# Two transformer-like blocks on one core: SSM products side by side, its input projection without the norm, rotation tables by state tile, and the SSM spread over more of block 1's projections

## The chip, the cores and the metric

The kernel runs on one core of a Trainium2 chip, as one program. TensorE does the matrix products, VectorE and ScalarE the elementwise work, SyncE (SP) issues the DMAs; each engine works through its own list of instructions in order. The metric is the device time of one execution in microseconds (us). Times of single instructions are from one execution that the hardware profiler recorded.

## The reference

Two blocks follow each other on 256 positions of width 1024, in float32. Block 1 is a hybrid layer:

```
n = rmsnorm(h, g_mix)                       # h * rsqrt(mean(h^2)) * g_mix
z = n @ w_in                                # q, k, v of 12 heads; u (512 wide); two gates (1024 each)
attn_d = dilated_attention(q, k, v) @ w_attn_proj
y = gelu(s5_ssm(u, ...))                    # 32 groups of 16 channels, 64 complex states each
ssm_d = (y @ w_glu_a) * sigmoid(y @ w_glu_b)
h = h + (gate_attn * attn_d + gate_ssm * ssm_d) @ w_out
h = h + (silu(n2 @ w_ffn_gate) * (n2 @ w_ffn_up)) @ w_ffn_down
h = h + sigmoid(h @ w_ple_gate) * (p @ w_ple_proj)
```

The SSM takes `u` through a matrix B per group into complex states, runs `h[t] = a * h[t-1] + (B u)[t]` over the 256 positions with a complex `a` per state, and reads `Re(C h) + D u`. Block 2 has two layers on the result and on a second sequence of 256 positions (a convolution module, then attention, each with an MLP), with gains and shifts from a conditioning vector.

## The kernel before

**Three products for one.** A float32 weight chunk of 128 x 1024 is loaded by DMA (tiles `r...`), ScalarE rounds it to a high part (`h...`), VectorE subtracts for the low part (`l...`), and TensorE makes three fast products with the high and low part of the other operand (`mm3`). `Stream.block` hands out 128 x 128 pieces and loads and splits the next chunk when one is used up. The streams are named after what they feed: `u`, `qkv` (with the products `pq` and `pv`), `gates` (`pgt`), `mix` (`m`), and so on.

**Block 1 up to the mix.** `Norm("n1")` sums squares of x (`ssn`), brings them into a column (`pcn`), takes the inverse root on VectorE and spreads it over all partitions (`bcn`). `gain_norm` makes `n_x`, the normed x in two parts (`nt`, `nh`, `nl`). From it come `u` (four products `pu`), then per head slot j the projections `slot_proj(j)` and the attention `slot_attn(j)`, and the gates. The stage `mix` needs the attention's result (`oh`, `ol`) and, in two of its three products, the SSM's result (`yh`, `yl`).

**The SSM.** `prelude` makes the step factors and rotation angles on VectorE. `ssm()` makes tables of rotations `tabs` by doubling (`cmul`, with `cm` as temporaries), and for each quarter q of the states combines two tables to the rotation of each position (`E`). For each of four state tiles of 128 states it multiplies `u` by B (`pb`, 32 rows of TensorE, real and imaginary part into one PSUM bank), rotates (`ab`, `gg`), runs the recurrence as VectorE scans, and rotates back (`DF`). Products with C (`py`, 32 columns of TensorE for each state tile) sum up the quarter, and a gelu gives `y`. Products in brackets of `together` are handed out as one piece, so that those in different rows or columns of TensorE can run beside each other.

**What sets the order.** Nothing runs as it is written down. Each call is recorded with a priority that counts up, and `Recorder.schedule` hands out the instructions for each engine from a cost table: the earliest priority whose operands and buffers are there, in the planner's own clock. The order that comes out is fixed when the program is built. Buffers are by tag: `S` and `Q` in SBUF, the PSUM banks `mm` (2), `at` (2), `ax`, `md`, `py` and `sb`. A section can be given priorities spread over a stretch: `ssm_part.spread(z0, z0 + (rec.prio - z0) * SSM_END)` lays the SSM over the first 0.8 of the priorities from the first projection to the last gate, so that its VectorE work stands between the projections' chunk splits.

Of the kernel before, what the change touches and what calls it, by code (L numbers as in the profile page):

```python
# [16 lines left out]
AF = mybir.ActivationFunctionType  # L17
# [76 lines left out]
GATES, SSM_END = (0, 0, 4, 12), 0.8  # L94
QA, QS = 3, 0.2
WO = ("mm", "at", "py", "sb")
# [386 lines left out]
def two_blocks(ctx: ExitStack, tc: tile.TileContext, I, out):  # L483
# [5 lines left out]
    def slot(name, shape, dt=FT, tag="S"):  # L489
        return rec.tile(tag, shape, dt, name)  # L490
# [54 lines left out]
    def load_feat(name, src, n=8):  # L545
        f = Feat(name, n)
        for i, t in enumerate(f.t):
            SP.dma_start(out=t, in_=src[:, 4 * i:4 * i + t.shape[1]])
        return f

    x0 = load_feat("x0", I["x"])
    SP.dma_start(out=cst, in_=I["cst"])
    SP.dma_start(out=prm, in_=I["prm"])
    pos = const("pos", [128, 2], I32)
    SP.dma_start(out=pos, in_=I["pos"])
# [207 lines left out]
    start = rec.prio  # L763
    nm = Norm("n1")
    for k in range(8):
        nm.add(x0[k])

# [92 lines left out]
    prelude()  # L860
    V.tensor_copy(identb, ident)
    for g in range(3):
        mf = tmp("mf", (128, 384))
        SP.dma_start(out=mf, in_=I["mask"][:, g])
        V.tensor_copy(mskb[:, g], mf)
# [14 lines left out]
    def ssm():  # L880
# [4 lines left out]
        V.memset(tabs[:, 0, :, 0, :], 1.0)  # L885
        V.memset(tabs[:, 1, :, 0, :], 0.0)
        for k in range(4):
            n = 1 << k
            for ab in range(2 if k < 3 else 1):
                o = 16 * (4 * ab + k)  # L890
                pc_ = cs[:, None, o:o + 16].to_broadcast([128, n, 16])
                ps_ = sn[:, None, o:o + 16].to_broadcast([128, n, 16])
                cmul(tabs[:, 0, ab, n:2 * n], tabs[:, 1, ab, n:2 * n], tabs[:, 0, ab, 0:n], tabs[:, 1, ab, 0:n],
                     pc_, ps_, (128, n, 16), "w")
        for q in range(4):
# [4 lines left out]
            ta = [tabs[:, i, 0, :, sq].rearrange("p b s -> p s b")[:, :, None, :].to_broadcast(full) for i in range(2)]  # L900
            tb = [tabs[:, i, 1, 0:8, sq].rearrange("p a s -> p s a")[:, :, :, None].to_broadcast(full) for i in range(2)]
            cmul(E[0], E[1], tb[0], tb[1], ta[0], ta[1], full, "w")
            for s2 in range(2):
                DF = []
                for s in (2 * s2, 2 * s2 + 1):
                    st = 4 * q + s
                    r = 32 * s
                    pb = bank("pb", (128, 2, T), "sb")
                    for ri in range(2):
                        PE.matmul(pb[:, ri], Bm[r:r + 32, q, ri, :], u[r:r + 32, q], start=True, stop=True,  # L910
                                  tile_position=(r, 0))
# [49 lines left out]
    z0 = rec.prio  # L961
# [870 lines left out]
```

## Time and profile before

| what | value |
|---|---|
| three runs, median (lowest to highest) | 1453.74 us (1450.98 to 1456.24) |
| the profiled execution, its own time | 1453.37 us |
| its span in the trace | 1451.6 us |
| TensorE (PE) busy, share of the span | 97% |
| VectorE (DVE) busy | 76% |
| ScalarE (ACT) busy | 48% |
| mean granted TensorE clock | 0.996 |

The span is the time from the first to the last instruction of the trace; the run's time has 1.8 us more around it. PE's busy share counts a matmul from its start to its modelled end, so matmuls that wait in the pipe count as well; how many start in a stretch says more. Line numbers of the trace are all L479, the line of the helper that hands out the instructions, so the rows are told apart by tile names. In a name, what stands before the arrow is written and what stands behind it is read.

### The profile page before, as it was taken

What the parts mean: (1) busy time and instruction counts of PE and PEld (TensorE: products, weight loads), DVE (VectorE), ACT (ScalarE), POOL (GpSimd) and SP (SyncE); (2) the same over time, 40 slices, a digit from 0 to 9 for tenths busy, and PEclk for the clock granted to TensorE, in tenths of its full rate; (3) what the DMA queues carried; (4) which work ended last, traced back from release to release, by engine and by line L of the source; (5) the groups of instructions that cost most, each with busy time, mean ns of one, the idle gap of its engine ahead of it and who ended that gap; (6) DMA issues with size and microseconds to landing.
All of it is one profiled execution on the core that took longest, in us unless ns stands there. A gap on an engine that the chain in (4) does not pass through costs nothing.

```text
span 1451.6 us, 26536 instructions
## 1 busy us (share of the span) xinstructions
PE 1414.4 (97%) x10436; PEld 1252.8 (86%) x10436; DVE 1101.1 (76%) x2244; ACT 703.7 (48%) x1233; POOL 1.9 (0%) x20
## 2 busy tenths in 40 slices
PE   6999999999999998999899999999999999999999
PEld 5888789998999998786699777778788987999998
DVE  7999995779999998585587986655444799777543
ACT  4544555554544445542265333333432569587532
POOL 0000000000000000000000000000000000000000
PEclk9999999999999999999999999999999999999999
DMA  8744455655565664679545776644232330366663
GB/s 329 262 160 130 161 157 158 188 174 177 187 189 180 188 197 148 218 244 308 183 139 171 228 243 220 217 145 132 87 91 70 91 114 31 117 178 186 188 194 98
DMA packets 78508, 249.58 MB, mean 172 GB/s; under 512 B 8496, under 2 KB 19248, under 8 KB 78384
## 3 DMA queue, kind: packets, MB, share of 16 engines
q1 hardware_dynamic: 78384, 247.89, 54.3%
q8 instruction: 82, 1.34, 0.4%
q14 instruction: 42, 0.34, 0.1%
HBM read 245.76 MB, written 2.10 MB: 171 GB/s over the span
## 4 chain that ended last, share of the span: by engine, by line
PE 82%; DVE 8%; DMA 6%; ACT 2%; issue 1%; SPq 0%; DVEq 0%; ACTq 0%
PE pf L479 33%; PE pq L479 5%; PE pd L479 4%; PE fu L479 4%; PE fg L479 4%; DMA rmod<-in_w_mod_dram 3%; PE p L479 3%; PE pgt L479 3%; PE pv L479 2%; PE m L479 2%; PE pg L479 2%; PE pa L479 2%; PE pw L479 2%; PE pe L479 1%; DVE ma L479 1%
## 5 line engine op out<-in xcount | busy, mean ns | idle before, releaser
L479 DVE TENSOR_TENSOR lffb<-rffb,hffb 128x1024 fp32r<-128x1024 f32 x64 | 78.4, 1225 | 87.9 <-ACT hffb L479 87.1
L479 ACT ACTIVATE hffb<-rffb 128x1024 fp32r<-128x1024 f32 x64 | 67.9, 1062 | 148.2 <-PE pf L479 145.5
L479 ACT ACTIVATE hffa<-rffa 128x1024 fp32r<-128x1024 f32 x64 | 68.0, 1062 | 122.4 <-PE pf L479 113.9
L479 DVE SCALAR_TENSOR_TENSOR ccv<-ucc,prm,ccv 128x241 f32<-128x241 f32 (+14 forms) x240 | 114.0, 475 | 4.0
L479 PE MATMUL pf<-eul,hffb 128*128 128x512 f32 (+1 forms) x288 | 107.4, 373 | 1.2 <-DVE xc L479 0.9
L479 PE MATMUL pf<-el,hffa 128*128 128x512 f32 (+1 forms) x288 | 106.9, 371 | 1.1 <-ACT hffa L479 1.1
L479 PE MATMUL pf<-euh,lffb 128*128 128x512 f32 (+1 forms) x288 | 106.9, 371 | 0.0
L479 PE MATMUL pf<-eh,hffa 128*128 128x512 f32 (+1 forms) x288 | 106.5, 370 | 0.0
L479 PE MATMUL pf<-eh,lffa 128*128 128x512 f32 (+1 forms) x288 | 106.5, 370 | 0.0
L479 PE MATMUL pf<-euh,hffb 128*128 128x512 f32 (+1 forms) x288 | 106.2, 369 | 0.0
L479 DVE TENSOR_TENSOR lffa<-rffa,hffa 128x1024 fp32r<-128x1024 f32 x64 | 78.2, 1224 | 19.9 <-ACT hffa L479 19.5
L479 ACT ACTIVATE hpw<-rpw 128x1024 fp32r<-128x1024 f32 x48 | 50.8, 1059 | 85.7 <-PE pg L479 24.4
L479 ACT ACTIVATE hqkv<-rqkv 128x1024 fp32r<-128x1024 f32 (+1 forms) x52 | 51.6, 993 | 57.7 <-PE pq L479 27.6
L479 ACT ACTIVATE hgu<-rgu 128x1024 fp32r<-128x1024 f32 x44 | 46.7, 1060 | 65.1 <-PE fu L479 29.2
L479 DVE SCALAR_TENSOR_TENSOR ma<-rmod,cvec,ma 128x1024 f32<-128x1024 f32 x56 | 71.0, 1282 | 8.5 <-DMA rmod<-in_w_mod_dram 8.3
L479 DVE SCALAR_TENSOR_TENSOR xT<-pf,mods,xT 128x256 f32<-128x256 f32 x72 | 34.6, 482 | 56.0 <-PE pf L479 56.0
L479 DVE TENSOR_TENSOR lpw<-rpw,hpw 128x1024 fp32r<-128x1024 f32 x48 | 58.5, 1221 | 21.5 <-ACT hpw L479 21.2
L479 PE MATMUL pf<-zh,hffa 128*128 128x258 f32 x256 | 72.4, 283 | 0.0
L479 PE MATMUL pf<-zl,hffa 128*128 128x258 f32 x256 | 72.4, 283 | 0.0
L479 PE MATMUL pf<-zh,lffa 128*128 128x258 f32 x256 | 72.3, 282 | 0.0
L479 PE MATMUL pf<-zuh,hffb 128*128 128x256 f32 x256 | 72.0, 281 | 0.0
L479 PE MATMUL pf<-zul,hffb 128*128 128x256 f32 x256 | 71.8, 281 | 0.0
(568 smaller groups left out, 4827.8 us busy)
## 6 DMA issues: line engine op xcount, KB each, us to landing
rmod<-in_w_mod_dram SPq DMA_DIRECT2D x96, 512.0 KB, 4.6
rffa<-in_w_ffa_dram SPq DMA_DIRECT2D x64, 512.0 KB, 3.6
rffb<-in_w_ffb_dram SPq DMA_DIRECT2D x64, 512.0 KB, 3.6
rpw<-in_w_pw_dram SPq DMA_DIRECT2D x48, 512.0 KB, 4.5
rgu<-in_w_gu_dram SPq DMA_DIRECT2D x44, 512.0 KB, 4.1
rqkv<-in_w_qkv_dram SPq DMA_DIRECT2D x36, 512.0 KB, 4.3
rdown<-in_w_down_dram SPq DMA_DIRECT2D x22, 512.0 KB, 3.9
rgates<-in_w_gates_dram SPq DMA_DIRECT2D x16, 512.0 KB, 3.6
```

The lines of the kernel that those rows point to most:

```text
L479: getattr(getattr(self.nc, op.eng), fn)(*map(real, args), **{k: real(v) for k, v in kw.items()})
```

## The change

1. x is loaded in halves behind the parameters, the first `u` chunk between them. The gain alone (`xgt`) is applied to x, split in two (`xgh`, `xgl`), and the four `pu` products use that; each sum stays in its own bank (`mm` and `at`) until the norm's factor is there, copied to SBUF (`bcs`), and VectorE multiplies by it into `u`. `n_x` is still made for the other projections.
2. `prelude` and the masks get priorities spread over `PRE` = 110, and the SSM starts its spread `PRE` later and ends at 0.9 instead of 0.8.
3. `tabs` has the state tile as the outer and the position as the inner index.
4. The B products of two state tiles are handed out together, on two banks (`sb` and `py`) and two row groups; the C products of all four state tiles of a quarter are handed out together, on four column groups, once instead of twice.

```diff
-GATES, SSM_END = (0, 0, 4, 12), 0.8
+GATES, SSM_END = (0, 0, 4, 12), 0.9
+PRE = 110
+SSM_PB = ('sb', 'py')
...
-    x0 = load_feat("x0", I["x"])
-    SP.dma_start(out=cst, in_=I["cst"])
     SP.dma_start(out=prm, in_=I["prm"])
+    x0 = Feat("x0")
...
+    xg = Pair("xg")
+    st_u = Stream("u")
+    for i, t in enumerate(x0.t):
+        SP.dma_start(out=t, in_=I["x"][:, 4 * i:4 * i + 4])
+        first = st_u.block() if not i else first
+        if not i:
+            SP.dma_start(out=cst, in_=I["cst"])
+    SP.dma_start(out=pos, in_=I["pos"])
     nm = Norm("n1")
     for k in range(8):
+        t = tmp("xgt", (128, T))
         nm.add(x0[k])
+        ts(t, x0[k], pp("g_mix", k), None, OP.mult)
+        split(t, *xg[k])
+    bc = nm.rstd()
+    pus = []
+    for m in range(4):
+        p = bank("pu", (128, T), ("mm", "at")[m % 2])
+        pus.append(p)
+        for k, x in enumerate(xg.all()):
+            mm3(p, st_u.block() if m or k else first, x, k == 0, k == 7)
...
-    bc = nm.rstd()
     n_x = gain_norm(x0, lambda k: pp("g_mix", k), bc, "n")
-    st_u = Stream("u")
     u = slot("u", [128, 4, T])
+    bcs = tmp("bcs", (128, T))
+    A.activation(bcs, bc, AF.Copy)
     for m in range(4):
-        p = bank("pu", (128, T))
-        lin(p, st_u, n_x)
-        A.activation(u[:, m], p, AF.Copy)
+        tt(u[:, m], pus[m], bcs, OP.mult)
...
+    pre_part.spread(rec.prio, rec.prio + PRE)
...
-                cmul(tabs[:, 0, ab, n:2 * n], tabs[:, 1, ab, n:2 * n], tabs[:, 0, ab, 0:n], tabs[:, 1, ab, 0:n],
-                     pc_, ps_, (128, n, 16), "w")
+                cmul(tabs[:, 0, ab, :, n:2 * n], tabs[:, 1, ab, :, n:2 * n], tabs[:, 0, ab, :, 0:n],
+                     tabs[:, 1, ab, :, 0:n], pc_, ps_, (128, 16, n), "w")
...
-            ta = [tabs[:, i, 0, :, sq].rearrange("p b s -> p s b")[:, :, None, :].to_broadcast(full) for i in range(2)]
-            tb = [tabs[:, i, 1, 0:8, sq].rearrange("p a s -> p s a")[:, :, :, None].to_broadcast(full) for i in range(2)]
+            ta = [tabs[:, i, 0, sq, :][:, :, None, :].to_broadcast(full) for i in range(2)]
+            tb = [tabs[:, i, 1, sq, 0:8][:, :, :, None].to_broadcast(full) for i in range(2)]
...
+                pbs = [bank("pb", (128, 2, T), tg) for tg in SSM_PB]
+                with rec.together(2):
+                    for ri in range(2):
+                        for s in range(2):
+                            r = 32 * (2 * s2 + s)
+                            PE.matmul(pbs[s][:, ri], Bm[r:r + 32, q, ri, :], u[r:r + 32, q], start=True, stop=True,
+                                      tile_position=(r, 0))
...
-                with rec.together(4):
-                    for i, (ci, d, ri) in enumerate(((0, 0, 0), (1, 1, 1), (2, 1, 0), (2, 0, 1))):
-                        for s in range(2):
-                            o = 2 * s2 + s
-                            PE.matmul(py[32 * o:32 * o + 32], Cp[ci][:, 4 * q + o, :], DF[s][:, d, ri],
-                                      start=i == 0, stop=i == 3, tile_position=(0, 32 * o))
+            with rec.together(4):
+                for i, (ci, d, ri) in enumerate(((0, 0, 0), (1, 1, 1), (2, 1, 0), (2, 0, 1))):
+                    for o in range(4):
+                        PE.matmul(py[32 * o:32 * o + 32], Cp[ci][:, 4 * q + o, :], DF[o][:, d, ri],
+                                  start=i == 0, stop=i == 3, tile_position=(0, 32 * o))
...
-    z0 = rec.prio
+    z0 = rec.prio + PRE
```

Since the planner sets the order, the lists of instructions show where things went. On VectorE at the end of the SSM (`lgates` and `lmix` are low parts of gate and mix chunks, `yl` the low part of the SSM's last quarter), before:

```order
L479 TENSOR_TENSOR lgates_507_2803<-rgates_505_2616,hgates_506_2787 128x1024
L479 TENSOR_TENSOR yl_92_2817<-ya_2741,yh_90_2798 128x256
L479 TENSOR_TENSOR lgates_511_2844<-rgates_509_2666,hgates_510_2833 128x1024
L479 TENSOR_TENSOR ol_223_2872<-sp_2622,oh_221_2863 128x256
L479 TENSOR_TENSOR lgates_515_2884<-rgates_513_2699,hgates_514_2869 128x1024
L479 TENSOR_TENSOR lgates_519_2917<-rgates_517_2727,hgates_518_2903 128x1024
L479 TENSOR_TENSOR lgates_523_2949<-rgates_521_2821,hgates_522_2936 128x1024
L479 TENSOR_TENSOR lgates_527_2981<-rgates_525_2858,hgates_526_2968 128x1024
L479 TENSOR_TENSOR lgates_531_3013<-rgates_529_2896,hgates_530_3000 128x1024
L479 TENSOR_TENSOR lmix_540_3044<-rmix_538_2929,hmix_539_3032 128x768
L479 TENSOR_TENSOR lmix_545_3076<-rmix_543_2961,hmix_544_3065 128x768
L479 TENSOR_TENSOR lmix_551_3108<-rmix_549_2993,hmix_550_3097 128x768
```

and after:

```order
L482 TENSOR_TENSOR lgates_544_3013<-rgates_542_2916,hgates_543_2989 128x1024
L482 TENSOR_TENSOR DF_3025<-gg_2940,E_2526 128x512
L482 TENSOR_TENSOR DF_3025<-gg_2940,E_2561 128x512
L482 TENSOR_TENSOR lmix_553_3042<-rmix_551_2944,hmix_552_3027 128x768
L482 TENSOR_TENSOR pl_1151_3062<-pT_920,ph_1150_2965 128x256 x2
L482 SCALAR_TENSOR_TENSOR yv_3068<-u_402,prm_67,py_3045 128x256
L482 TENSOR_SCALAR ya_3079<-ya_3079 128x256
L482 TENSOR_TENSOR ya_3079<-ya_3079,yv_3068 128x256
L482 TENSOR_TENSOR lmix_558_3105<-rmix_556_2981,hmix_557_3091 128x768
L482 SCALAR_TENSOR_TENSOR ya_3079<-yt_3101,yv_3068 128x256
L482 TENSOR_TENSOR yl_105_3128<-ya_3079,yh_103_3122 128x256
L482 TENSOR_TENSOR lmix_564_3145<-rmix_562_3001,hmix_563_3132 128x768
```

Before, six gate chunks and all mix chunks stood behind `yl`; after, no gate chunk, and of the mix only from the third chunk on.

On TensorE, the start of the last sum with C (`py`) and what stands ahead of it, before (`s` and `sp` are scores of the attention; further gate products follow behind the sum):

```order
L479 LDWEIGHTS identb_101
L479 MATMUL s_476_2697<-mskb_342,identb_101 128x256
L479 MATMUL sp_2622<-qk_425_2414,qk_424_2271 128x256
L479 MATMUL py_2495<-DF_2584,Cp_17_584 32x256
L479 MATMUL py_2495<-DF_2695,Cp_17_584 32x256
```

and after (a `pgt` product is one of the gates):

```order
L482 MATMUL pgt_3023<-nh_59_304,hgates_535_2907 128x256
L482 MATMUL pgt_3023<-nh_59_304,lgates_536_2962 128x256
L482 MATMUL py_3045<-DF_2669,Cp_52_743 32x256
L482 MATMUL py_3045<-DF_2794,Cp_52_743 32x256
L482 MATMUL py_3045<-DF_2913,Cp_52_743 32x256
L482 MATMUL py_3045<-DF_3025,Cp_52_743 32x256
```

Before, a sum reads two states (`DF`) and stands within the attention, with gate groups still to come; now it reads four and stands among the products of the last gate group: 60 gate products and 12 products `m<-ol`, `m<-oh` come between it and the first `m<-yl`. Behind that point TensorE's list is the same as before up to the products `pe` at the end of block 1, but for a few neighbours that changed places.

At the start of TensorE's list, before:

```order
L479 MATMUL ssn_8_96<-sqn_12_91,cst_74 32x256 x2
L479 MATMUL pcn_24_139<-cst_74,rown_25_130 128x1 x2
L479 MATMUL bcn_30_190<-cst_74,nw_167 128x128 x2
L479 MATMUL pu_213<-nl_33_205,hu_46_136 128x256
L479 MATMUL pu_213<-nh_31_200,hu_46_136 128x256
```

and after:

```order
L482 MATMUL pu_131<-xgl_10_114,hu_13_121 128x256
L482 MATMUL pu_131<-xgh_8_105,hu_13_121 128x256
L482 MATMUL ssn_15_140<-sqn_17_98,cst_80 32x256 x2
L482 MATMUL ssn_15_140<-sqn_18_116,cst_80 32x256 x2
L482 MATMUL pu_131<-xgh_8_105,lu_14_133 128x256
```

The products `pu` moved ahead of the norm's sums; `pcn` and `bcn` stand among them.

## Rows read from the trace of the kernel before

**Rows 1.** Windows view: us:us length, then busy us (instructions) of each engine, clock, DMA.

```profile
0.00:20.00 20.00, 8.34 (x43) 6.69 (x43) 12.34 (x69) 11.63 (x23) 0.20 (x4) 1.00 0.89 338
20.00:60.00 40.00, 39.19 (x294) 33.92 (x294) 38.33 (x136) 17.94 (x32) 0.00 (x0) 1.00 0.88 302
60.00:220.00 160.00, 157.90 (x1080) 128.61 (x1079) 156.44 (x365) 78.46 (x170) 0.00 (x0) 0.99 0.48 158
220.00:260.00 40.00, 39.94 (x330) 37.96 (x330) 20.99 (x36) 21.84 (x46) 0.00 (x0) 1.00 0.50 153
...
340.00:540.00 200.00, 200.00 (x1694) 200.00 (x1694) 191.59 (x343) 93.79 (x132) 0.00 (x0) 1.00 0.61 187
540.00:760.00 220.00, 204.87 (x1806) 171.81 (x1806) 153.78 (x323) 99.15 (x188) 1.66 (x16) 0.98 0.66 205
```

**Rows 2.** Tile view of `yl`: duration ns min/median/max, first and last start us, form.

```profile
L479 DVE TENSOR_TENSOR yl<-ya,yh x4: 403/420/431, 108.6 to 231.8; 128x256 fp32r<-128x256 f32 x4
```

**Rows 3.** Timeline of VectorE near 234 us: start, us, instruction, [idle before <-releaser].

```profile
234.01 1.23 DVE L479 TENSOR_TENSOR lgates<-rgates,hgates 128x1024 fp32r<-128x1024 f32 x1 [1.74 <-ACT hgates L479]
```

**Rows 4.** Timeline of the start: VectorE and TensorE.

```profile
7.81 0.37 DVE L479 TENSOR_SCALAR prm<-prm 128x16 f32<-128x16 f32 x2 [0.46 <-DMA prm<-in_prm_dram]
...
12.91 1.19 PE L479 MATMUL bcn<-cst,nw 128*128 128x128 f32 x4 [2.18 <-DVE nw L479]
...
15.79 0.58 PE L479 MATMUL pu<-nl,hu 128*128 128x256 f32 x1 [1.70 <-DVE nl L479]
...
33.06 0.38 PE L479 MATMUL pq<-nl,hqkv 128*128 128x256 f32 x1 [0.76 <-ACT u L479]
```

**Rows 5.** Lines by form, VectorE, 20 to 240 us: busy us, mean ns | idle before.

```profile
L479 DVE TENSOR_TENSOR ab<-pb,E 128x512 f32<-128x512 f32 x32 | 21.7, 683 | 0.4 <-PE pb L479 0.4
L479 DVE TENSOR_TENSOR cm<-tabs 128x512 f32<-128x512 f32 x16 | 16.5, 1054 | 0.0
L479 DVE TENSOR_TENSOR E<-cm,cm 128x512 f32<-128x512 f32 x8 | 5.5, 688 | 0.0
L479 DVE TENSOR_TENSOR cm<-tabs,trig 128x16 f32<-128x16 f32 (+3 forms) x28 | 4.8, 206 | 0.2
L479 DVE TENSOR_TENSOR tabs<-cm,cm 128x16 f32<-128x16 f32 (+3 forms) x14 | 2.9, 208 | 0.2
L479 DVE TENSOR_TENSOR c<-Cm,ssc 128x512 f32<-128x512 f32 x4 | 2.7, 686 | 0.0
L479 DVE TENSOR_TENSOR cm<-tabs,trig 128x16 f32<-128x16 f32 x8 | 1.2, 171 | 0.0
L479 DVE TENSOR_TENSOR cm<-tabs,trig 128x128 f32<-128x128 f32 x4 | 1.1, 285 | 0.0
L479 DVE TENSOR_SCALAR ya<-ya 128x256 f32<-128x256 f32 x4 | 1.1, 285 | 0.0
```

**Rows 6.** Timeline of VectorE, 14 to 18 us: three low parts in a row.

```profile
15.32 1.09 DVE L479 TENSOR_TENSOR nl<-nt,nh 128x256 fp32r<-128x256 f32 x3
```

**Rows 7.** Timeline of TensorE at four places.

```profile
68.30 1.10 PE L479 MATMUL pb<-u,Bm 32*128 32x256 f32 x4 [1.03 <-DVE ab L479]
69.33 0.40 PE L479 MATMUL pq<-nh,hqkv 128*128 128x256 f32 x1
...
85.61 1.92 PE L479 MATMUL py<-DF,Cp 128*32 128x256 f32 x16
87.46 0.33 PE L479 MATMUL ptp<-cst,P 128*128 128x128 f32 x1
...
260.43 0.28 PE L479 MATMUL m<-yl,hmix 128*128 128x256 f32 x1
...
260.79 0.28 PE L479 MATMUL m<-yl,hmix 128*128 128x256 f32 x1
...
1179.05 0.50 PE L479 MATMUL S<-k1l,q1h 64*128 64x512 f32 x2
1179.39 0.40 PE L479 MATMUL S<-k1h,q1h 64*128 64x512 f32 x2
```

More of the change, by code (lines that the diff above doesn't have):

```diff
@@ L549, in load_feat @@
         return f
-    x0 = load_feat("x0", I["x"])
-    SP.dma_start(out=cst, in_=I["cst"])
     SP.dma_start(out=prm, in_=I["prm"])
+    x0 = Feat("x0")
     pos = const("pos", [128, 2], I32)
-    SP.dma_start(out=pos, in_=I["pos"])
     def pp(n, i=0, w=1):
@@ L846, in prelude @@
         stt(Cp[2], t3, -1.0, t4, OP.mult, OP.subtract)
-    bc = nm.rstd()
     n_x = gain_norm(x0, lambda k: pp("g_mix", k), bc, "n")
-    st_u = Stream("u")
     u = slot("u", [128, 4, T])
+    bcs = tmp("bcs", (128, T))
+    A.activation(bcs, bc, AF.Copy)
     for m in range(4):
-        p = bank("pu", (128, T))
-        lin(p, st_u, n_x)
-        A.activation(u[:, m], p, AF.Copy)
+        tt(u[:, m], pus[m], bcs, OP.mult)
     SP.dma_start(out=Bm, in_=I["bm"])
     SP.dma_start(out=Cm, in_=I["cm"])
[L860 to L865, printed above, removed]
+    pre_part = rec.section()
+    with pre_part:
+        prelude()
+        V.tensor_copy(identb, ident)
+        for g in range(3):
+            mf = tmp("mf", (128, 384))
+            SP.dma_start(out=mf, in_=I["mask"][:, g])
+            V.tensor_copy(mskb[:, g], mf)
+    pre_part.spread(rec.prio, rec.prio + PRE)
     yx = Pair("y", 4, tag="Q")
@@ L884, in ssm @@
         tabs = slot("tabs", [128, 2, 2, 16, 16])
-        V.memset(tabs[:, 0, :, 0, :], 1.0)
-        V.memset(tabs[:, 1, :, 0, :], 0.0)
+        V.memset(tabs[:, 0, :, :, 0], 1.0)
+        V.memset(tabs[:, 1, :, :, 0], 0.0)
         for k in range(4):
@@ L890, in ssm @@
                 o = 16 * (4 * ab + k)
-                pc_ = cs[:, None, o:o + 16].to_broadcast([128, n, 16])
-                ps_ = sn[:, None, o:o + 16].to_broadcast([128, n, 16])
-                cmul(tabs[:, 0, ab, n:2 * n], tabs[:, 1, ab, n:2 * n], tabs[:, 0, ab, 0:n], tabs[:, 1, ab, 0:n],
-                     pc_, ps_, (128, n, 16), "w")
+                pc_ = cs[:, o:o + 16, None].to_broadcast([128, 16, n])
+                ps_ = sn[:, o:o + 16, None].to_broadcast([128, 16, n])
+                cmul(tabs[:, 0, ab, :, n:2 * n], tabs[:, 1, ab, :, n:2 * n], tabs[:, 0, ab, :, 0:n],
+                     tabs[:, 1, ab, :, 0:n], pc_, ps_, (128, 16, n), "w")
         for q in range(4):
@@ L899, in ssm @@
             full = [128, 4, 8, 16]
-            ta = [tabs[:, i, 0, :, sq].rearrange("p b s -> p s b")[:, :, None, :].to_broadcast(full) for i in range(2)]
-            tb = [tabs[:, i, 1, 0:8, sq].rearrange("p a s -> p s a")[:, :, :, None].to_broadcast(full) for i in range(2)]
+            ta = [tabs[:, i, 0, sq, :][:, :, None, :].to_broadcast(full) for i in range(2)]
+            tb = [tabs[:, i, 1, sq, 0:8][:, :, :, None].to_broadcast(full) for i in range(2)]
             cmul(E[0], E[1], tb[0], tb[1], ta[0], ta[1], full, "w")
+            DF = []
             for s2 in range(2):
-                DF = []
+                pbs = [bank("pb", (128, 2, T), tg) for tg in SSM_PB]
[5 more added lines that the diff above has]
+                                      tile_position=(r, 0))
                 for s in (2 * s2, 2 * s2 + 1):
                     st = 4 * q + s
[L907 to L911, printed above, removed]
+                    pb = pbs[s % 2]
                     Ec, Es = (e[:, s].rearrange("p a b -> p (a b)")[:, None, :].to_broadcast([128, 4, H]) for e in E)
```

## The prediction

> **What bounds the kernel now.** I read the windows view first, cutting the span where the ratio of the engines changes [rows 1]. From 340 to 540 us TensorE has no idle time and starts 1694 matmuls in 200 us; from 60 to 220 us it starts 1080 in 160 us, which is 6.8 per us against 8.5, although its busy share is nearly as high (a matmul that waits in the pipe counts as busy). VectorE is busy for 156.44 of those 160 us. So block 1's projections are paced by VectorE, which cuts every weight chunk into two parts (the `l...` tiles) and does the whole SSM beside it. Then it turns: between 220 and 260 us VectorE is busy for 20.99 of 40 us, and TensorE starts 330 matmuls, 8.3 per us. The tile view of the SSM's result says why [rows 2]: its last part, `yl`, is written at 231.8 us, and its first reader, the product `m<-yl`, starts at 260.43 us [rows 7]. The SSM is finished 28 us too early; VectorE is short of time before, and has 19.0 us to spare after. The waits there are short ones for ScalarE's first half of the next chunk, one for each gate chunk [rows 3].
>
> At the start TensorE does little until 15.79 us [rows 4]: the inputs land, the norm's sums go through TensorE, VectorE, TensorE (12.91 us), and only then can the first normed operand be made.
>
> **How the sum is made.** Everything that the change touches lies before the first `m<-yl`. From the lists of instructions, what stands behind it is in the same order on TensorE up to the end of block 1, and later with small swaps. So I work out when that product starts and carry the shift to the end: behind it TensorE is full from 340 to 540 us, and VectorE (191.59 of 200) has what it needs. The sum stands against the profiled execution: 1453.37 us, its span 1451.6 and 1.8 around it; the median of the three runs, 1453.74, is 0.4 above.
>
> **VectorE's work up to the third `lmix`** (before: it ends at 258.1 us, as [rows 1] add up to 228.1 us of work by 260 and 31.9 of idle time). The lists name the same instructions in both kernels up to that row, but for these:
> - Rotation tables by state tile. Sixteen products `cm<-tabs` of 512 elements take 1054 ns each; their sums `E<-cm,cm`, of the same size, take 688 [rows 5]. The long ones read a table with a step of 16 elements, which the new layout makes 1; `c<-Cm,ssc` repeats one element 32 times and still takes 686, so the repeated operand isn't what costs. I take 688: 16 x 0.366 = -5.9 us. Bounds: -5.9 and 0.
> - The building of the tables (28 + 14 instructions, 4.8 + 2.9 us [rows 5]) now writes and reads runs of 1, 2, 4 and 8 elements with a step of 16 between them. No row has such runs. Bounds: 0, and the long products' ratio on all of it, 7.7 x 0.54 = +4.1. Most of the time of so small an instruction doesn't depend on its size (171 ns at 16 elements, 285 at 128), so I take a quarter: +1.1. The Trainium skill (SBUF — State Buffer, section Door 1: The DMA port swizzle) says that SBUF is read in lines of 16 bytes, and that each access to a new line pays. The trace agrees for the step of 64 bytes, 1054 ns against 688; by that rule runs of 1 and 2 elements would pay as well, which speaks against this half of the edit.
> - The input projection without the norm adds 8 scalings by the gain, 8 low parts and 4 multiplications by the norm's factor. Three low parts in a row take 1.09 us [rows 6], 0.36 each: 12 x 0.36 = +4.3; a scaling of that size takes at most 0.285: 8 x 0.25 = +2.0. ScalarE gets 8 high parts and gives up 4 copies; it is at half load there, and VectorE covers it.
>
> Sum +1.5: 229.6 us. So VectorE has no less to do. It does it at another time.
>
> **VectorE's idle time.** Before: 7.7 us up to 20, 1.7 up to 60, 3.6 up to 220, 19.0 up to 260 [rows 1].
> - Start: the parameters are first in SP's queue, not fourth, and the gain products need only the first half of x, so VectorE starts near 5 us and not at 7.8 [rows 4]. But the second half of x is now behind a weight chunk and the constants (512 KB more ahead of it, some 1.4 us), and VectorE waits for it once. I take 6.5 us for 7.7.
> - 20 to 220 us: 5.3, as before. The SSM's products with B now come in pairs on two banks, and each pair waits until VectorE has read the pair before. Before, VectorE waited 0.4 us in all for these products [rows 5], so I add nothing.
> - The hole of 19.0 us goes. The lists show the place: before, the last `yl` has six gate chunks and all mix chunks behind it; after, no gate chunk, and of the mix only from the third chunk on.
> - At the very end four dependent steps with two trips to ScalarE stand almost alone; I take 2.5 us (before, a single wait for ScalarE there was 1.74 us [rows 3]).
>
> 229.6 + 6.5 + 5.3 + 2.5 = 243.9 us for the third `lmix`. The last SSM state is ready 5 us of work and those 2.5 us earlier, at 236.4.
>
> **TensorE behind it.** In the new order the last `py` stands in TensorE's queue ahead of 60 gate products and 12 mix products, so these wait for it. Products of 256 columns start 0.12 us apart (`m` from 260.43 to 260.79, three steps), a group of `py` takes 1.85 [rows 7]: 72 x 0.12 + 1.9 = 10.5. The first `m<-yl` starts at 246.9 instead of 260.4: **-13.5 us**.
>
> **Side by side, costed at nothing.** The B products of one state tile (four records) take 1.03 us until the next product [rows 7]; 16 state tiles are 16.5 us, in pairs 8.2 less. A group of `py` takes its 1.85 us on two column groups; the eight of them become four of that length, on four: 7.4 less. That pairs in different rows run together is seen in block 2: six `S` products of two row groups start as three pairs (the first two are shown, 0.34 us apart [rows 7]). So TensorE loses 15.6 us of work. At the start it begins near 8 us, but the projections proper still need the normed x, which comes 4 us later (the norm's sums wait for the second half of x), so they start near 28 and not at 33.06 [rows 4]: -5. TensorE alone would allow `m<-yl` at 260.4 - 15.6 - 5 = 239.8 or sooner, which is before VectorE's 246.9: the saving is hidden behind VectorE's work. It isn't idle: without it TensorE would need 255.4 less the waits that the spreading ends, so it is worth 0 to 9 us as cover.
>
> **Downstream** the 15 us that TensorE idles from 540 to 760 us [rows 1] stay; the small swaps there I give 0, with 3 us either way.
>
> Forecast: 1453.4 - 13.5 = 1439.9, and 0.4 for the median: **1440 us** in round numbers. Its own range: idle at the start 5, 4 later and tables at 0 give 5 us less, and 3 from downstream: 1432; tables at +4.1 give 3 more, 3 more idle, 3 downstream: 1449 at the outside, 1446 for most of it.
>
> **Rivals.**
> - *TensorE becomes the bound.* VectorE keeps ahead (its idle time in the middle goes, since TensorE no longer holds it up), and `m<-yl` starts at 239.8: -20.6, 1433 us or a little less. For it: the 15.6 us are real work. Against it: the last `py` would have to start at 229.4, by when VectorE has 224.6 us of work (229.6 less the 5 behind it) and could idle for less than 5. Chance 0.1.
> - *The layout gives nothing, or the tables cost what the step of 64 bytes costs.* +5.9 or +3.0 on VectorE, which is the bound, so all of it counts: 1443 to 1449. For it: no row shows the new runs. Against it: 686 ns for `c<-Cm,ssc`. By the Trainium skill (SBUF — State Buffer, Door 1: The DMA port swizzle) the lines of 16 bytes would bring the cost of the tables, not the lack of a gain. Chance 0.13.
> - *The gain is given back:* 10 to 14 us come back, as waits behind the start (everything of x's second half is later) and in the last SSM quarter, whose lateness now counts at once, since TensorE's queue has nothing but it to wait for. Between 1449.4 and 1458. Chance 0.09.
> - *Slower: handshakes.* `py` now needs four states at once and shares a bank with the second product of each pair, so at 8 pairs and 4 sums TensorE stands still in its queue until VectorE has come that far, and VectorE then waits for TensorE's products. If both wait 2 us at each of 12 places, the stage grows by 24 - 13.5: 1464. It decides from 1.5 us at each place, where 18 - 13.5 leaves 4.5. Against it: in the lists VectorE has 2 to 10 us of other rows between a `py` and the pair behind it, and before, waits of this kind came to 0.4 us. Chance 0.07.
> - *The pairs don't run together.* +8.2 on TensorE only: 239.8 becomes 248.0, one us behind VectorE's 246.9: 1441. It lies within the forecast.
>
> **Chances.** The forecast's own band, 1432 to 1446, holds 0.61. About 0.3%, or 4.4 us, is what a measurement of this kernel tells from no change, so faster is below 1449.4: 0.61 + 0.10 + 0.13 = 0.84; within 0.3%: 0.09; slower: 0.07. The range 1431 to 1449 leaves out the two last cases and a tail at the fast end.
>
> **What would show it.** Right: VectorE busy for over 95% from 20 to 235 us and no hole until the mix; the last `yl` within 5 us of the first `m<-yl`, which starts at 243 to 250 us; `cm<-tabs` of 512 elements near 690 ns; B products starting in pairs a few ns apart; TensorE still short of its full rate between 60 and 220 us; the full stretch that begins at 340 us begins at 326. Wrong: VectorE idle in the middle of the stage, next to TensorE waiting; table products of 128 elements far above 285 ns; the first `pq` later than 30 us; new idle time of TensorE between 326 and 526 us.

## The result, and the profile after

| | before | changed |
|---|---|---|
| median (lowest to highest), four runs each | 1453.51 us (1450.98 to 1456.24) | 1431.14 us (1430.71 to 1432.74) |
| profiled execution, its own time | 1453.37 us | 1432.74 us |
| its span | 1451.6 us | 1430.9 us |
| mean granted TensorE clock | 0.996 | 0.996 |

The ratio is 0.9848, with a 95% interval of 0.9828 to 0.9867: 22 us faster (19 to 25). Measured again beside a later experiment the ratio was 0.9823 (0.9804 to 0.9841). The forecast was 1440 us, 13.5 us faster.

The windows view of the changed kernel, columns as in [rows 1]:

```profile
0.00:20.00 20.00, 10.94 (x58) 8.87 (x59) 14.19 (x70) 11.15 (x24) 0.20 (x4) 1.00 0.85 319
20.00:60.00 40.00, 39.95 (x304) 35.10 (x303) 38.86 (x124) 22.16 (x39) 0.00 (x0) 1.00 0.83 288
60.00:220.00 160.00, 154.04 (x1185) 133.35 (x1184) 157.04 (x398) 85.67 (x186) 0.00 (x0) 0.99 0.53 175
220.00:260.00 40.00, 38.83 (x342) 37.56 (x341) 30.71 (x57) 21.50 (x41) 0.00 (x0) 1.00 0.67 204
...
340.00:540.00 200.00, 200.00 (x1683) 199.63 (x1682) 191.84 (x341) 91.47 (x128) 0.00 (x0) 1.00 0.60 185
```

VectorE (the third pair of numbers) now has work from 220 to 260 us as well, 30.71 us for 20.99, and TensorE starts 1185 matmuls from 60 to 220 us for 1080. The timeline of TensorE shows the places of [rows 4] and [rows 7]: start, duration, instruction, [idle before and what ended it].

```profile
28.48 0.39 PE L482 MATMUL pq<-nl,hqkv 128*128 128x256 f32 x1
...
205.07 1.13 PE L482 MATMUL pb<-u,Bm 32*128 32x256 f32 x8
206.13 0.38 PE L482 MATMUL pgt<-nl,hgates 128*128 128x256 f32 x1
...
232.74 1.93 PE L482 MATMUL py<-DF,Cp 128*32 128x256 f32 x32
234.60 0.39 PE L482 MATMUL pgt<-nl,hgates 128*128 128x256 f32 x1
...
243.17 0.28 PE L482 MATMUL m<-oh,lmix 128*128 128x256 f32 x1
244.62 0.39 PE L482 MATMUL m<-yl,hmix 128*128 128x256 f32 x1 [1.17 <-ACT gt L482]
```

Eight records of `pb` take 1.06 us until the next product, where four took 1.03; 32 of `py` take 1.86, where 16 took 1.85. So both run side by side at no extra time. For `py` TensorE saves the 7.4 us of the prediction, for `pb` more than its 8.2. The prediction takes 1.03 us for each of the 16 state tiles, but before only five of them had their four records in a row. Eleven had them in two groups of two, with other products between, and such a group takes 0.62 us until the next product:

```profile
33.73 0.69 PE L479 MATMUL pb<-u,Bm 32*128 32x256 f32 x2
34.35 0.39 PE L479 MATMUL pq<-nh,lqkv 128*128 128x256 f32 x1
```

Added up over the groups, `pb` took 19.2 us before and takes 8.5 now: 10.7 us saved, with `py` some 18 for the 15.6 of the prediction. VectorE's timeline beside it has the last state and the third `lmix`:

```profile
231.25 1.29 DVE L482 TENSOR_TENSOR DF<-gg,E 128x512 f32<-128x512 f32 x2
...
240.01 0.96 DVE L482 TENSOR_TENSOR lmix<-rmix,hmix 128x768 fp32r<-128x768 f32 x1 [0.65 <-ACT hmix L482]
```

The last state is ready at 232.5 us, and TensorE comes to the sum that reads it at 232.7: the two engines arrive at the same moment. Where the 20.6 us between the two profiled executions lie is read from the first start of four tiles:

| first start, us | before | changed | shift |
|---|---|---|---|
| `m<-yl`, the mix with the SSM | 260.4 | 244.6 | -15.8 |
| `pe<-xl`, end of block 1 | 577.5 | 561.3 | -16.2 |
| `pf<-el`, block 2's first MLP | 752.4 | 733.0 | -19.4 |
| the end (own time) | 1453.4 | 1432.7 | -20.6 |

I call 577 to 752 us, from `pe` to `pf`, the late stretch. It gained 3.2 us, and the forecast had nothing there.

### The profile page after: what moved, and what is told of

It reads as the page before. It is cut to its first block, busy times and chain, and to the rows that moved or that the text cites. A ratio compares the mean times of both kernels' runs of the same rounds, so it can differ in the third digit from the quotient of the medians.

```text
span 1430.9 us, 26557 instructions
## 1 busy us (share of the span) xinstructions
PE 1393.1 (97%) x10436; PEld 1243.9 (87%) x10436; DVE 1100.6 (77%) x2264; ACT 705.5 (49%) x1238; POOL 1.9 (0%) x20
## 4 chain that ended last, share of the span: by engine, by line
PE 75%; DMA 3%; DVE 2%; ACT 1%; issue 1%; SPq 0%; DVEq 0%; ACTq 0%
PE pf L482 36%; PE fg L482 4%; PE pd L482 4%; PE fu L482 4%; PE p L482 3%; PE m L482 2%; PE pa L482 2%; PE pg L482 2%; PE pq L482 2%; PE pw L482 2%; PE pe L482 2%; DMA ud<-ucl 1%; PE pt L482 1%; PE po L482 1%; DMA rmod<-in_w_mod_dram 1%; PE S L482 1%
## 5 line engine op out<-in xcount | busy, mean ns | idle before, releaser
L482 DVE TENSOR_TENSOR lffa<-rffa,hffa 128x1024 fp32r<-128x1024 f32 x64 | 78.2, 1225 | 19.7 <-ACT hffa L482 19.4
L482 PE MATMUL pf<-zuh,lffb 128*128 128x256 f32 x256 | 71.7, 280 | 0.0
```

What stands on the lines that cost most here:

```text
L482: getattr(getattr(self.nc, op.eng), fn)(*map(real, args), **{k: real(v) for k, v in kw.items()})
```

## Experiments

Three theories stand in the expectations. V is the prediction's: VectorE's work decides when the first `m<-yl` starts, and what TensorE saves is hidden. T is its opposite. B: both lists are full, and the later one decides. All ratios are to the kernel before on the same chip; the start of `m<-yl` is from the profiled execution and varies little (244.6 and 243.5 us in two executions of the changed kernel, 241.3 and 241.5 in two of another).

### Each part taken out of the changed kernel

Rotation tables back in the old layout:

```diff
-            ta = [tabs[:, i, 0, sq, :][:, :, None, :].to_broadcast(full) for i in range(2)]
+            ta = [tabs[:, i, 0, :, sq].rearrange("p b s -> p s b")[:, :, None, :].to_broadcast(full) for i in range(2)]
...
```

> The changed kernel with the rotation tables in the old layout (position outer, state tile inner), nothing else. VectorE gets its 16 long table products at 1054 ns back for 687: +5.9 us of work, all of it before the last SSM state. Theory V (the prediction's: VectorE's lane alone sets when the first m<-yl starts): all 5.9 us come back, 1437 us. Theory T (TensorE's own queue sets it, VectorE has time to spare): 0 to 1 us, 1431 to 1432. Theory B (both lanes end together, as the trace of the changed kernel reads: the last state is ready at 232.5 us and TensorE reaches the sum that reads it at 232.7): 4 to 6 us, 1435 to 1437, the same as V.

Measured: 1435.98 us, ratio 0.9869 (0.9846 to 0.9891), 4.8 us above the changed kernel's median (3 to 7 by the ratios of its two measurements); `m<-yl` at 248.8, 4.2 later. V and B hold, T falls: VectorE has next to no time to spare in the changed kernel.

B products singly, C products for two state tiles at a time:

```diff
-                pbs = [bank("pb", (128, 2, T), tg) for tg in SSM_PB]
-                with rec.together(2):
...
+                    pb = bank("pb", (128, 2, T), "sb")
...
```

> The changed kernel with the B products of one state tile at a time and the C products of two, as before. TensorE gets 15.6 us of work back (8.2 for B, 7.4 for C), VectorE none. Theory V: TensorE's saving was cover behind VectorE's work, so 0 to 9 us come back, most likely 3: 1431 to 1440. Theory T: all of it less the waits that it fills, 12 to 15.6 us: 1443 to 1447. Theory B: also 10 to 15.6 us, since TensorE has no slack from 160 us on (its queue loses under 3 us from there to the first m<-yl): 1441 to 1447.

Measured: 1451.98 us, ratio 0.9968 (0.9948 to 0.9987): most of the gain is lost, more than any of the theories has. `m<-yl` starts at 253.8 us, 9.2 later, where V's 0 to 9 and the 10 of B meet; the rest of the loss lies in the late stretch, 183.6 us long for 171.7. (The profiled execution, 1455.28 us, is the slowest of the ten, 3.3 above their median.)

The input projection on the normed x, and the loads in their old order:

```diff
-            mm3(p, st_u.block() if m or k else first, x, k == 0, k == 7)
...
+        lin(p, st_u, n_x)
+        A.activation(u[:, m], p, AF.Copy)
...
```

> The changed kernel with the input projection on the normed x, and the order of the loads, as before. VectorE loses 6.7 us of work (scalings, low parts, products with the factor) and idles some 2 us more at the start; TensorE starts pu 6 to 7 us later and its full list 4.6 us later (33.1 for 28.6). Theory V: VectorE's lane ends 4 to 5 us sooner, 1426 to 1428. Theory T: TensorE starts its list 4.6 us later and has it all to give back: 1435 to 1436. Theory B: the later lane counts, 1434 to 1436.

Measured: 1427.68 us, ratio 0.9818 (0.9794 to 0.9841); `m<-yl` at 241.3 us, 3.3 sooner, as V has it. This looked like a kernel that beats the changed one, so both went to one chip again:

> The changed kernel once more, to stand beside the next one on the same chip: 1430 to 1434 us.

> The changed kernel with the input projection on the normed x and the order of loads as before, once more, beside the changed kernel on the same chip. Theory V (VectorE's 6.7 us for the input projection without the norm cost more than the earlier start of TensorE brings): 2 to 5 us sooner than the changed kernel. Rival: the first comparison was noise, and both take the same time within 1 us; then the first m<-yl of the two also starts within 1 us. Rival 2: the 4.6 us of earlier start come through, and it is 1 to 4 us later.

Measured: 1430.69 us (0.9823, 0.9804 to 0.9841) and 1430.49 us (0.9822, 0.9800 to 0.9844). The times are the same, though `m<-yl` again starts sooner with the norm back (241.5 us for 243.5). So up to the mix this part of the change costs 2 to 3 us; in the whole, nothing that these runs can measure.

The spreading undone:

```diff
-GATES, SSM_END = (0, 0, 4, 12), 0.9
+GATES, SSM_END = (0, 0, 4, 12), 0.79
...
-    pre_part.spread(rec.prio, rec.prio + PRE)
...
-    z0 = rec.prio + PRE
+    z0 = rec.prio
```

> The changed kernel with the spreading undone: the prelude where it stood, the SSM laid over the first 0.79 of the priorities (0.79 and not 0.8, a neighbour of the old value). The work of both engines stays. Theory V: VectorE is short before and idles behind the SSM again, with a hole of 10 to 19 us: 1441 to 1448. Theory T: the order matters less than TensorE's work, whose 15.6 us stay saved; up to 5 us come back: 1431 to 1436. Theory B: VectorE's hole returns and TensorE waits for it in the middle, 8 to 14 us: 1439 to 1445. Beside it: the stretch behind block 1 gave 3 us in the changed kernel (the shift grows from 16.2 to 19.4 us between 577 and 720 us); if that comes from the planner's order there and not from the edits, it will differ by some us in each of these four kernels.

Measured: 1445.18 us, ratio 0.9934 (0.9909 to 0.9958); `m<-yl` at 256.0, 11.4 later; its last `yl` is written at 223.8 us. V and B hold. The old value was 0.8 and not 0.79; what this small step does by itself no run shows.

### Each part alone on the kernel before

The edits are the same hunks, the other way round; the side-by-side products alone have 0.79 for 0.8 beside them.

> The kernel before with the spreading alone (prelude over 110 priorities, SSM from there to 0.9). The work of both engines is that of before. Theory V (VectorE's lane alone sets the first m<-yl): its hole of 19 us goes, and the product starts 11 to 14 us sooner: 1440 to 1443 us. Theory B (two lanes, the later one counts): TensorE still has its 15.6 us of single products; with the side-by-side products undone in the changed kernel the first m<-yl started at 253.9 us, and here TensorE's projections start 5 us later than there, so 0 to 5 us sooner than before: 1449 to 1454 us. Since the stretch from 577 to 720 us moved by -7 to +8 us in the kernels so far, with the granted clock and the waits there, the start of m<-yl is to be read beside the time.

Measured: 1455.93 us, ratio 1.0003 (0.9987 to 1.0020); `m<-yl` at 257.1, 3.3 sooner. V falls: VectorE's hole is filled as in the changed kernel (30.21 us busy from 220 to 260 us), but the gain doesn't come. Over the whole way from 20 us to `m<-yl` VectorE still idles for 18.6 us and TensorE for 2.4 (windows view). B's 0 to 5 us hold.

> The kernel before with the B products in pairs and the C products of four state tiles together, nothing else but 0.79 for 0.80 in the SSM's spread (a neighbour). TensorE has 15.6 us less to do, VectorE the same. Theory V: VectorE paces the stage up to the SSM's end and idles behind it as before, so TensorE waits longer: 0 to 2 us, 1452 to 1454. Theory T (TensorE's work counts): 12 to 15 us sooner, 1438 to 1442. Theory B: the lane that is later is VectorE's with its hole; 0 to 4 us, 1450 to 1454.

Measured: 1441.72 us, ratio 0.9914 (0.9884 to 0.9943); `m<-yl` at 260.0, 0.4 sooner, as V and B have it. Yet the whole is 12 us faster, as T has it. The profiled execution is 10.1 us shorter, nearly all of it behind `m<-yl` and 8.7 us in the late stretch, 166.2 us for 174.9; none of the theories had it.

> The kernel before with the rotation tables by state tile alone. VectorE has 16 x 0.367 = 5.9 us less to do, all in the stage that it paces. Theory V: all of it is gained, 1447 to 1449. Theory T: nothing, 1452 to 1455. Theory B: between, 2 to 6 us, since TensorE's waits there add up to 15.6 us and VectorE ends first anyhow: 1447 to 1451.

Measured: 1454.05 us, ratio 0.9991 (0.9973 to 1.0008); `m<-yl` at 258.3, 2.1 sooner. V falls again: 5.9 us less work on VectorE bring 2 up to the mix, and in time nothing that can be measured. B's 2 to 6 us hold for the start alone.

> The kernel before with the input projection without the norm and its order of loads alone. VectorE has 6.7 us more to do and idles about 2 us less at the start; TensorE starts its list of projections 4.6 us sooner. Theory V: 3 to 5 us later, 1456 to 1459. Theory T: up to 4.6 us sooner, 1449 to 1451. In the changed kernel taking it out gained 3.4 us up to the first m<-yl, as V has it; here VectorE paces the stage even more, so V is expected.

Measured: 1466.88 us, ratio 1.0076 (1.0045 to 1.0106). `m<-yl` at 259.9, 0.5 sooner, between V and T; the loss of 11 us is in the late stretch, 189.2 us long for 174.9 (what is in it stands below).

### What the list of waits says

Spread, pairs and tables alone bring 3.3 + 0.4 + 2.1 = 5.8 us up to `m<-yl`; together, in the kernel with the norm back, they bring 19.1. (No run has the spreading and the pairs alone together.) The reason is in a view that I hadn't put into the prediction, the waits of TensorE from 60 to 260 us. Kernel before (what waited, for what, us in all, times, longest):

```profile
PE pb L479 <- DVE ab L479: 1.0, 1, 1.0
PE pv L479 <- ACT pk L479: 0.7, 1, 0.7
PE sp L479 <- ACT P L479: 0.2, 1, 0.2
```

and with the side-by-side products alone, the first rows of it:

```profile
PE pq L480 <- DVE lqkv L480: 2.2, 2, 1.2
PE ptp L480 <- ACT PT L480: 1.4, 3, 0.6
PE pm L480 <- DMA rmod<-in_w_mod_dram: 1.3, 2, 1.1
PE pq L480 <- ACT pk L480: 1.2, 1, 1.2
```

Before, TensorE waited for 1.9 us in 200. It was full; the shorter products make it wait. They also let other work in: 32 more records of `pm` (explained below) stand ahead of `m<-yl`, some 5 us of TensorE. The windows from 20 us to the first `m<-yl` tell the same for five kernels (columns as in [rows 1]). Before:

```profile
20.00:220.00 200.00, 197.09 (x1372) 162.53 (x1372) 194.76 (x500) 96.40 (x201) 0.00 (x0) 0.99 0.56 186
220.00:260.40 40.40, 40.34 (x333) 38.36 (x333) 21.39 (x36) 22.06 (x46) 0.00 (x0) 1.00 0.51 155
```

Side by side alone:

```profile
20.00:220.00 200.00, 189.96 (x1413) 158.35 (x1415) 196.37 (x507) 98.80 (x205) 0.00 (x0) 0.99 0.59 199
220.00:260.00 40.00, 38.95 (x336) 37.33 (x336) 19.38 (x29) 21.70 (x44) 0.00 (x0) 1.00 0.59 198
```

The changed kernel without the side-by-side products:

```profile
20.00:220.00 200.00, 198.26 (x1394) 164.89 (x1392) 189.35 (x503) 104.18 (x220) 0.00 (x0) 1.00 0.57 193
220.00:253.80 33.80, 33.80 (x280) 31.05 (x280) 25.25 (x50) 15.80 (x30) 0.00 (x0) 1.00 0.51 160
```

The changed kernel without the spreading:

```profile
20.00:220.00 200.00, 185.56 (x1396) 155.39 (x1395) 195.84 (x526) 100.61 (x211) 0.00 (x0) 0.97 0.58 194
220.00:256.00 36.00, 35.77 (x302) 35.28 (x300) 16.86 (x26) 20.12 (x41) 0.00 (x0) 1.00 0.61 199
```

The changed kernel:

```profile
20.00:232.50 212.50, 206.49 (x1592) 180.95 (x1591) 208.41 (x544) 114.58 (x235) 0.00 (x0) 0.99 0.59 197
232.50:244.60 12.10, 10.95 (x107) 9.68 (x105) 5.73 (x12) 6.13 (x15) 0.00 (x0) 1.00 0.83 258
```

Length less busy time gives TensorE's idle time from 20 us to `m<-yl`: 3.0 us before, 1.7 with single products and the spreading, 11.1 with pairs alone, 14.7 with pairs and no spreading, 7.2 with both. VectorE's: 24.2, 19.2, 24.2, 23.3 and 10.5. With single products TensorE is full, and VectorE may do its work when it likes. With pairs and the old order VectorE is full until the SSM's end (196.37 us of 200) and idle behind it, and TensorE waits. Only with both does the way to `m<-yl` get much shorter; in the kernel with the norm back TensorE idles for 3.4 us of it and VectorE for 10.9. This is theory B.

These waits cost more than their length. Without the spreading the granted clock from 20 to 220 us is 0.97, for 0.99 in the changed kernel. By an estimate from these means, 0.02 of 200 us, some 4 us of the 11.4 are clock. The last section shows how a wait and the clock stand together.

### The late stretch

In the kernels above the late stretch lasts from 166.2 to 189.2 us, though no edit is in it. The products `pm` of the conditioning vector, each set of 8 records with 1 MB of weights, are what the planner puts in where, by its cost table, TensorE has time. Records of `pm` up to `m<-yl`, up to `pe` and in the late stretch (windows of `pm` alone), before:

```profile
0.00:260.40 260.40, 10.91 (x80) 1.62 (x80) 0.66 (x2) 0.99 0.58 193
260.40:577.50 317.10, 2.13 (x16) 0.32 (x16) 0.00 (x0) 1.00 0.60 183
577.50:752.40 174.90, 15.88 (x96) 2.31 (x96) 1.32 (x4) 0.99 0.69 216
```

The changed kernel:

```profile
0.00:244.60 244.60, 12.13 (x88) 1.86 (x88) 0.66 (x2) 0.99 0.62 210
244.60:561.30 316.70, 3.20 (x24) 0.47 (x24) 0.00 (x0) 1.00 0.59 186
561.30:733.00 171.70, 12.67 (x80) 1.94 (x80) 1.30 (x4) 0.99 0.67 207
```

Side by side alone, the first and the last of the three:

```profile
0.00:260.00 260.00, 15.96 (x112) 2.35 (x112) 0.66 (x2) 0.99 0.61 210
...
576.00:742.20 166.20, 10.60 (x64) 1.52 (x64) 0.66 (x2) 0.99 0.67 202
```

With pairs alone, 32 records were done ahead of `m<-yl` that were done in the late stretch before, in time that TensorE would have waited, and the late stretch is 8.7 us shorter. The clock doesn't explain it: the granted clock of the late stretch is 0.99 in both kernels. To see whether the count is the cause, `pm` alone was moved, by its priorities:

```diff
-MOD1 = (0.5, 1.0)
+MOD1 = (-4.0, 0.0)
```

> The kernel before with nothing of the change, but the products pm of the conditioning vector's second group placed earlier by their priorities (MOD1 = (-4.0, 0.0) for (0.5, 1.0)). In the instruction lists the records of pm ahead of the first m<-yl stay 80; from there to the end of block 1 (the first pe) they become 56 for 16; in the late stretch, from the first pe to the first pf<-el, 56 for 96. In the ten kernels measured so far that late stretch lasts 166.2 us with 64 records of pm, 168.1 to 172.1 with 80, 174.9 to 183.6 with 96, 178.6 with 104 and 189.2 with 112, whatever edit was in it. Theory M (pm with its 1 MB of weights per 8 records is a filler; what is not done early has to be done in the late stretch, where it waits for its loads): the late stretch falls to 163 to 167 us, the middle one grows from 317.1 by the pm's own work, 5 x 1.07 = 5.4 us, and the whole comes out 3 to 7 us sooner, 1447 to 1451. Theory C (the late stretch varies by clock and by chance, the counts go with it by accident): only the own work moves, late stretch 168 to 185 us, the whole within 2 us of before or worse.

Measured: 1452.02 us, ratio 0.9976 (0.9962 to 0.9991). The windows of `pm` behind `m<-yl`:

```profile
262.40:586.20 323.80, 7.46 (x56) 1.10 (x56) 0.66 (x2) 0.99 0.61 195
586.20:753.30 167.10, 10.86 (x56) 1.59 (x56) 0.66 (x2) 0.99 0.63 194
```

The late stretch fell by 7.8 us, to the upper end of what M expects, and the middle one grew by 6.7, a little over its 5.4; `m<-yl` itself starts 2 us later. In the profiled execution nothing is left; by the ratio 3.5 us are (1.3 to 5.5), as M has it and C has not. So the count is a cause, and 40 records are worth some 8 us there, as far as one profiled execution of each kernel tells. That M's middle stretch was expected at the records' bare time was too cheap.

The count isn't the only one. The late stretch before and with the input projection alone, all instructions:

```profile
577.50:752.40 174.90, 164.00 (x1489) 133.89 (x1488) 114.12 (x243) 75.50 (x137) 1.51 (x15) 0.99 0.69 216
```

```profile
577.80:767.00 189.20, 176.40 (x1530) 142.67 (x1529) 115.21 (x239) 74.98 (x135) 1.55 (x16) 0.95 0.69 216
```

The second has 112 records of `pm` for 96 and is 14.3 us longer. Its granted clock is 0.95 for 0.99: 0.05 of 189.2 us is 9.5, 0.01 of 174.9 is 1.7, so by this estimate half of the difference is clock. With the side-by-side products taken out there are 96 records as before, 183.6 us and a clock of 0.97. Why the clock is lower in these two no run here shows.

The same in the kernel with the norm back, with MOD1 = (-2.0, 0.5):

> The changed kernel with the input projection on the normed x as before (the fastest kernel so far), and pm's second group earlier (MOD1 = (-2.0, 0.5)): 96 records of pm ahead of the first m<-yl as without it, 40 for 16 in the middle stretch, 56 for 80 in the late one. Theory M: late stretch 163 to 166 us for 168.1, middle 317.8 + 3 x 1.07 = 321.0, net 0 to 3 us sooner than that kernel: 1424 to 1428. Theory C: late stretch only 3 us shorter by the own work or not at all, net 0 to 5 us later: 1428 to 1433.

Measured: 1431.59 us, ratio 0.9836 (0.9816 to 0.9856): no gain, as C has it for the time. The late stretch is 165.8 us (168.1 and 173.6 without the move), the middle one 321.1 (317.8 and 316.5): the stretches are those of M, and they cancel against the faster of the two executions without the move. (The profiled execution, 1427.15 us, is the fastest of the four.) Moving `pm` out of the late stretch paid most where TensorE would have waited, as with the pairs alone, and little where it went into a stretch in which TensorE is full.

None of these kernels is measurably faster than the changed one.

## Why the prediction was right, and where it was wrong

The direction was right, and the time lies at the very edge of the range that was given, 1431 us. That it lies inside is luck: the three terms that are to make the sum 5 us less at its low end, idle time at the start, idle time later and the tables, are 1.5 + 1.3 + 1.1 = 3.9, so that the sum itself reaches down to 1433. The forecast was 8.9 us too high: 2.3 up to `m<-yl`, 0.4 to the end of block 1, 3.2 in the late stretch, 1.2 behind it, and 1.6 by which the profiled execution lies above the median (0.2 are rounding).

**VectorE's sum held.** By form, from 0 to 265 us in the changed kernel (busy us, mean ns | idle before):

```profile
L482 DVE TENSOR_TENSOR cm<-tabs 128x512 f32<-128x512 f32 x16 | 10.9, 687 | 0.0
L482 DVE TENSOR_TENSOR xgl<-xgt,xgh 128x256 fp32r<-128x256 f32 x8 | 2.9, 421 | 0.0
L482 DVE TENSOR_SCALAR xgt<-x,prm 128x256 f32<-128x256 f32 x8 | 2.3, 350 | 1.2 <-DMA x<-in_x_dram 1.2
L482 DVE TENSOR_TENSOR u<-pu,bcs 128x256 f32<-128x256 f32 x4 | 1.5, 428 | 0.0
L482 DVE TENSOR_TENSOR cm<-tabs,trig 128x16 f32<-128x16 f32 x8 | 1.1, 174 | 0.1
L482 DVE TENSOR_TENSOR cm<-tabs,trig 128x128 f32<-128x128 f32 x4 | 1.1, 288 | 0.0
```

The table products fell from 1054 ns [rows 5] to 687, for which 688 was taken. The new input projection costs 2.9 + 2.3 + 1.5 = 6.7 us for 6.3. The building of the tables was put at +1.1 and costs next to nothing (174 and 288 ns for 171 and 285): of the bounds 0 and 4.1 the lower was right. Single elements with a step of 64 bytes do cost something: the writes `tabs<-cm,cm` of 16 elements take 183 ns for 174 (185 with the tables alone; 172 and 175 in two other kernels with the old layout). By an estimate from the long products, 0.7 ns more per element (1054 less 687, over 512), 16 elements would pay 11 ns. The rule of the Trainium skill on lines of 16 bytes (SBUF — State Buffer, section Door 1: The DMA port swizzle) also says that two accesses to a line are enough for the full rate, so that of the runs of 1 and 2 that the prediction names only those of 1 would pay. The trace agrees as far as it goes: the writes of 32 elements, where a run is two, take 182 and 193 ns in the new layout and 182 to 192 in the old. So the rule isn't refuted; on so small an instruction it is worth very little. The work up to the third `lmix` is 228.1 us, for 229.6.

**The idle time was a little less.** 5.8 us at the start for 6.5 and 4.1 from 20 to 220 us for 5.3 (both from the first windows above); 0.5 us more stands at the very end. The third `lmix` ends at 241.0 for 243.9, the last state at 232.5 for 236.4, and the products `pq` start at 28.48 for "near 28".

**TensorE behind it** was put at 10.5 us from the last state to `m<-yl`. It took 10.7 to the last product ahead of it (232.5 to 243.2), and then came a wait of 1.17 us that the prediction doesn't have: by the row above it waited for ScalarE's `gt`, which reads the last gate; ScalarE had it in its list behind squares (`sqca`) that had waited 1.98 us for a load (ScalarE's timeline, at 242.23). The first `m<-yl` was expected at 246.9 and started at 244.6.

**The step that failed is the reading of what bounds the stage before.** The prediction says that projections are paced by VectorE because TensorE starts only 6.8 matmuls per us from 60 to 220 us, and sets its busy share of 157.90 us in 160 [rows 1] aside. The busy share was right. The stage holds `pv` products of 384 columns, some 160 of the 1080, which start 0.175 us apart, and `pb` records at 0.26 to 0.31 us each, where a product of 256 columns takes 0.12:

```profile
61.67 0.34 PE L479 MATMUL pv<-hqkv,nh 128*128 128x384 f32 x1
61.85 0.34 PE L479 MATMUL pv<-lqkv,nh 128*128 128x384 f32 x1
```

So the rate falls without any wait; the list of waits has 1.9 us. Both engines were full up to 220 us. From this the second failed step follows: the side-by-side products were "costed at nothing", worth 0 to 9 us as cover. They save some 18 us of TensorE's work and not 15.6, as shown above. Taken out they cost 9.2 us up to `m<-yl` (just beyond the end of that range) and by the ratios 17 to 21 of the 22 us in time. The spreading, to which the sum gave the hole's 19 us, gains 3.3 us up to `m<-yl` alone and nothing in time.

**The term that is missing is the late stretch.** The prediction saw "small swaps" in TensorE's list there and gave them 0, with 3 us either way. They were two sets of `pm`, one of which is now done ahead of `m<-yl` and one in the middle stretch. At some 8 us for 40 records (the run with `pm` moved alone) 16 records are worth 3.1; 3.2 was measured, and 4.7 in the changed kernel's second execution (170.2 us). Two executions of one kernel can differ by more in this stretch, as shown below, so this agreement shows little.

**The rivals.** "TensorE becomes the bound" gave 1433 us, the nearest number, but not the mechanism: VectorE's work still counts (`m<-yl` 4.2 us later without the new tables). The two came out together at 232.5 and 232.7 us. No handshake cost showed, and the wait of VectorE for the pairs is 0.3 us. The layout gave its full gain per instruction, and what the prediction set down as its worth in time, 5.9 us, is 3 to 7 when it is taken out and not measurable when it is put in alone.

**The signs.** Most of those that the prediction set down came. VectorE is busy for 98% (208.41 of 212.5 us), the table products take 687 ns, the first `pq` starts ahead of 30 us; the last `yl` starts 5.7 us ahead of `m<-yl`, for "within 5". That TensorE starts fewer matmuls than at its full rate between 60 and 220 us (7.4 per us for 8.5) was to show that VectorE paces it. It doesn't show that, for the reason given above.

## What to carry to other kernels

Whether an engine is the bound of a mixed stage is told by its idle time and its list of waits, not by how many matmuls start per microsecond; tiles of other shapes lower that rate without a wait. Where two engines are both full, an edit on one of them shows little alone and its whole worth together with the other, so such parts have to be tried together, and taken out one at a time. And where a planner sets the order, time that is freed in one stage is filled with work from a later one: count what moved across the stage's end, and look for the gain there. Read the granted clock next to the idle time: in these traces waits of TensorE cost more than their length, where the clock fell with them.

## What the runs showed of the hardware

The granted clock differs between executions of one program. The kernel with the norm back was profiled twice; from 598 to 640 us the windows view has, in the first execution and in the second:

```profile
598.00:640.00 42.00, 41.74 (x424) 35.49 (x422) 34.97 (x69) 17.33 (x28) 0.62 (x6) 1.00 0.89 275
```

```profile
598.00:640.00 42.00, 38.07 (x370) 31.61 (x372) 32.58 (x63) 16.23 (x25) 0.42 (x4) 0.94 0.88 258
```

TensorE was idle for 3.9 us of the second and for 0.3 of the first, its mean clock was 0.94 for 1.00 (between its levels of 2.4 and 1.2 GHz), and it started 54 matmuls fewer in the same 42 us; the late stretch as a whole lasted 173.6 us for 168.1. Here the idle time came first. Two sets of 48 products (`cvp`) of the second execution, and the windows view up to and from the fall of the clock:

```profile
627.13 2.77 PE L482 MATMUL cvp<-usl,cwl 128*32 128x256 f32 x48
...
636.26 5.35 PE L482 MATMUL cvp<-usl,cwl 128*32 128x256 f32 x48 [3.67 <-DMA rpw<-in_w_pw_dram]
```

```profile
628.00:634.80 6.80, 4.59 (x57) 3.46 (x49) 5.31 (x10) 1.46 (x3) 0.21 (x2) 1.00 1.08 282
634.80:641.70 6.90, 5.44 (x49) 2.65 (x49) 0.03 (x1) 0.00 (x0) 0.00 (x0) 0.51 0.97 276
```

TensorE waited from 632.6 to 636.3 us for what the profile puts down to a load. Near 634.8, within the wait, the granted clock falls from 1.00 to the lower level, and the 48 products behind it take 5.35 us, for 2.80 in the first execution. So a wait of 3.7 us cost 2.6 more through the clock, and both together are more than the 5.5 us between the two stretches. The kernel before has the same on a smaller scale: behind the wait of 1.03 us ahead of `pb` [rows 7] the granted clock is 0.54 from 69.3 to 73.0 us, and `pq` products start 0.21 us apart for 0.12. A gain of 3 us that shows in one profile of this stretch alone isn't to be relied on.

The other is in the products: in different row groups or column groups of TensorE twice as many records took 1.06 us for 1.03 (`pb`) and 1.86 for 1.85 (`py`), so side by side was free to within 3%. Two records of `pb` between other products took 0.62 us, so a state tile in two such groups cost 1.24 us, for the 1.03 of four records in a row.
